# One level of Strassen's method in both feed-forward blocks of a two-layer encoder trunk

## The chip, the cores and the metric

The kernel runs on one core of one Trainium2 chip. The metric is the device time of one execution in microseconds (us); several executions are timed and their median is taken. Engines: PE (TensorE, matrix products; PEld is its weight load), DVE (VectorE), ACT (ScalarE), POOL (GpSimd) and SP (SyncE, which issues most transfers). Each engine takes its instructions in order, and waits for others by semaphores.

## The reference

`x` is 512 tokens of 1024 features, in float32. Two layers, each with two sub-layers, and each sub-layer does `x = x + RMSNorm_post(f(RMSNorm_pre(x)))`. The first sub-layer is a mixer (layer 0: forgetting attention and pooling; layer 1: a gated linear recurrence). The second one is the feed-forward block, and it is the one that changes:

```python
def swiglu(h, w_gate, w_up, w_down):
    return (jax.nn.silu(h @ w_gate) * (h @ w_up)) @ w_down
```

`w_gate` and `w_up` are 1024 x 2816, `w_down` is 2816 x 1024.

## The kernel before

One program, in the order mixer 0, feed-forward 0, mixer 1, feed-forward 1. Every float32 product a.b is carried as three products of a shorter type (float32r): ah.bh + ah.bl + al.bh, where ah holds the upper bits and al = a - ah the rest (`mm3`, L123 to L127). So each operand exists as a high and a low tile, and a third of a block product is one matrix instruction.

**Weights** stream from memory in units of [128, 1024] (512 KB), in the order of use. `unit()` (L153) hands out the next one and first has `prefetch` (L146) bring in two more. `split_weights` (L139) does it for one: SP issues the load into a `raw` buffer (three of them), ACT casts it into `whi`, DVE subtracts to get `wlo` (four pairs). These three are put ahead of other work in the scheduler (`tc.high_priority`). In the profile every DVE instruction stands under L89, the helper that records it.

**The activations** h lie transposed, as 8 tiles of features by 512 tokens, high (`hTh`) and low (`hTl`).

**Gate and up** (`ffn`, L689): 22 column tiles of 128 for each. The first four products run in halves of 256 tokens (`split_proj`, L674), since token blocks 2 and 3 come later from the mixer; the other 40 take 512 tokens, 8 k-steps of 3 instructions each. Per tile pair: Silu on ACT (L706), a product on DVE, a cast on ACT (L709) and a subtraction on POOL (L710) that makes the low part.

**Down**: 22 units; `TokenMajor` (L510) accumulates four token blocks by two halves of the features in the eight banks of PSUM. The last six units are held back and used token block by token block (`finish`), so that `Finish` (L556) can normalize one block while the next one is multiplied: `half` takes squares on ACT and scales on DVE, `block` takes the root on POOL (`pow`, L553), adds to x (`xres`), and does the next norm, which `second` and `transpose` queue behind a given amount of PE work (`later`, `tick`, L107 to L116). `need` forces them when their result is called for.

PE's order is the order of the program text, as those helpers leave it.

Of the kernel before, what the change touches and what calls it, by code (L numbers as in the profile page):

```python
# [7 lines left out]
F32 = mybir.dt.float32  # L8
# [13 lines left out]
FT = FF // P  # L22
EPS = 1e-6
# [3 lines left out]
# columns of the packed per-partition constants and parameters  # L27
# [23 lines left out]
# shape constants: identity | causal mask | zeros, upper triangle with the diagonal, ones  # L51
# [7 lines left out]
def tile_trunk(ctx: ExitStack, tc: tile.TileContext, cst_d, sh_d, xw_d, x_d, gains_d, pw_d, w_d, out_d):  # L59
    """Every float32 product a.b is carried as ah.bh + ah.bl + al.bh on float32r,  # L60
    where ah holds the top 12 bits of a and al = a - ah the rest, exactly."""
# [9 lines left out]
    def f32(ap):  # L71
        return ap.bitcast(F32)
# [6 lines left out]
    class Recorded:  # L79
        """an engine that remembers the last instruction given to it"""  # L80
# [21 lines left out]
    # work for the tensor engine that is queued behind `delay` us of other work of it,  # L102
    # while what it needs is being made
# [19 lines left out]
    def mm3(out, ah, al, bh, bl, start, stop, us=0.65):  # L123
        nc.tensor.matmul(out, lhsT=ah, rhs=bh, start=start, stop=False)  # L124
        nc.tensor.matmul(out, lhsT=ah, rhs=bl, start=False, stop=False)  # L125
        nc.tensor.matmul(out, lhsT=al, rhs=bh, start=False, stop=stop)  # L126
        tick(us)  # L127

# [4 lines left out]
    NU = w_d.shape[0]  # L133
# [5 lines left out]
    def split_weights(src, n, hi, lo):  # L139
        raw = pw.tile([P, D], F32, name="raw", tag="raw", bufs=3)  # L140
        with tc.high_priority():
            nc.sync.dma_start(out=raw[:, :n], in_=src)
            nc.scalar.copy(out=hi, in_=raw[:, :n])  # L143
            vec.tensor_sub(out=lo, in0=raw[:, :n], in1=f32(hi))

    def prefetch(n):  # L146
        while state["loaded"] < min(NU, state["used"] + n):
            hi, lo = place.get(state["loaded"], whl)()
            split_weights(w_d[state["loaded"]], D, hi, lo)
            ready.append((hi, lo))  # L150
            state["loaded"] += 1

# [27 lines left out]
    # the tensor engine's clock rises while the first loads are under way  # L180
# [9 lines left out]
    def log1p(out, e, u, d):  # L190
        """out = log(1 + e) for 0 <= e <= 1, with what the rounding of 1 + e takes off; u and d are scratch."""
# [7 lines left out]
    # ================= layer 0 mixer =================  # L199
# [4 lines left out]
    # values and forget gates, k outermost, on x*g; the row scale is applied on the way out.  # L204
    # columns: even heads, gates | odd heads
# [4 lines left out]
    for k in range(KT):  # L210
        xw = pw.tile([P, T + 520], F32, name="raw", tag="raw", bufs=3)
# [36 lines left out]
    # row scale of the first norm  # L248
# [41 lines left out]
    # -8 softplus(-lam)  # L290
# [4 lines left out]
    # c = cumsum(log f), as rows 32*b + 4*h + r for every b and r, by a product with the triangle  # L295
# [10 lines left out]
    def gates():  # L306
# [12 lines left out]
        # c[t] - c[s] as the product of rows c_hi[t], c_lo[t], 1, 1 and 1, 1, -c_hi[s], -c_lo[s]  # L319
# [40 lines left out]
    split_weights(pw_d, T, pwt[:, 0], pwt[:, 1])  # L360
# [106 lines left out]
    def transposes(pr):  # L467
        # s blocks 0 | 1 | zeros, 3, 2 of the transposed probabilities
# [19 lines left out]
    def values(h, parts):  # L488
# [8 lines left out]
        # the products of the values' low parts lie on the other half of the partitions  # L497
# [12 lines left out]
    class TokenMajor:  # L510
        """out[t, :] += a[k].T @ w[k] over the k of `srcs`; one bank per (token block, half of the features)."""
# [43 lines left out]

    class Finish:  # L556
        """Post-norm, residual, next pre-norm and its transpose, a token block at a time."""

        def __init__(self, n):
            self.gpost = gtile()  # L560
            nc.sync.dma_start(out=self.gpost, in_=gains_d[2 * n:2 * n + 1, :].broadcast_to([P, D]))
            self.gpre = None
            if n < 3:
# [4 lines left out]
        def half(self, i, hf, acc):  # L568
            if hf == 0:
                self.u[i] = (small(2), tmp())  # L570
            ss, u = self.u[i]
            cs = slice(hf * T, (hf + 1) * T)
            nc.scalar.activation(out=junk[:, cs], in_=acc, func=AF.Square, scale=1.0 / 32, accum_out=ss[:, hf:hf + 1])  # L573
            vec.tensor_mul(out=u[:, cs], in0=acc, in1=self.gpost[:, cs])

        def block(self, i):
# [27 lines left out]
            def transpose():  # L604
                h = box["h"]
# [292 lines left out]
```

## Time and profile before

| what | us |
|---|---|
| runs | 1100.03, 1100.60, 1099.24 |
| median | 1100.03 |
| span of the profiled execution, first to last instruction | 1097.0 |
| what lies around that span, by the median | 3.0 |
| PE busy | 1079.5 (98%) |
| PE weight loads, beside the products | 893.5 |
| DVE busy | 485.1 (44%) |
| ACT busy | 421.3 (38%) |
| POOL busy | 139.7 (13%) |

The share of busy time says which engine has no room left; the chain of waits says what the end hung on. A PE row in the timeline gives its start and its own duration; rows overlap in the pipeline, so the cost of one instruction is the distance between starts. The granted clock of PE is 0.997 of its upper level (2.4 GHz) over the span.

### The profile page before, as it was taken

The page shows a single profiled execution, that of the slowest core. Times are in us where ns is not written, and L with a number is a line of the kernel's source. Part 1 is how long each engine was busy: PE and PEld are TensorE (multiplying, and loading weights), DVE is VectorE, ACT ScalarE, POOL GpSimd, SP SyncE. Part 2 cuts the span into 40 slices and gives each one's busy share as a digit, 9 for nine tenths or more (in the row PEclk, how much of TensorE's full clock was granted, in tenths as well). Part 3 has the DMA queues.
Part 4 walks back from the last instruction along what each step waited for, and adds up shares of the span by engine and source line. Part 5 has one row for each costly group of instructions (what it writes and reads, how often), then busy time and mean ns, then how long its engine had stood idle before and what let it go on. Part 6 is the DMA issues. An engine that isn't in the chain of part 4 may idle for free.

```text
span 1097.0 us, 12987 instructions
## 1 busy us (share of the span) xinstructions
PE 1079.5 (98%) x5166; PEld 893.5 (81%) x5166; DVE 485.1 (44%) x665; ACT 421.3 (38%) x659; POOL 139.7 (13%) x140
## 2 busy tenths in 40 slices
PE   8999999999999999999999999999999999999997
PEld 7878787988888888888898887898888888888885
DVE  4899856522222222224348598543222222222323
ACT  6767634422222222114235984433222222221211
POOL 0020201111111111000003104101111111110000
PEclk9999999999999999999999999999999999999999
DMA  8644343322222222226113223313222222223401
GB/s 287 179 112 106 97 155 114 115 95 90 90 93 95 96 96 96 96 96 193 57 39 116 96 86 106 116 40 130 89 92 94 96 96 96 96 81 111 135 24 72
DMA packets 33292, 114.37 MB, mean 104 GB/s; under 512 B 4048, under 2 KB 4048, under 8 KB 33232
## 3 DMA queue, kind: packets, MB, share of 16 engines
q1 hardware_dynamic: 32656, 111.45, 31.1%
q10 hardware_dynamic: 576, 2.10, 0.5%
q8 instruction: 40, 0.66, 0.2%
q14 instruction: 20, 0.16, 0.0%
HBM read 107.24 MB, written 2.10 MB: 100 GB/s over the span
## 4 chain that ended last, share of the span: by engine, by line
PE 83%; DVE 8%; ACT 3%; issue 2%; DMA 2%; POOL 0%; SPq 0%; DVEq 0%; POOLq 0%; ACTq 0%
PE ps L125 27%; PE ps L124 27%; PE ps L126 27%; DVE wlo L89 2%; DVE tmp L89 2%; DVE cr L89 2%; DVE th L89 1%; ACT whi L143 1%; PE ps L610 1%; DMA tmp<-in_sh 1%; PE ps L475 1%; PE ps L495 1%; ACT th L774 1%; PE ps L447 0%; DMA raw<-in_xw 0%
## 5 line engine op out<-in xcount | busy, mean ns | idle before, releaser
L124 PE MATMUL ps<-hTh,whi 128*128 128x512 f32 (+1 forms) x1024 | 382.8, 375 | 0.2 <-DVE vs L89 0.2
L125 PE MATMUL ps<-hTl,whi 128*128 128x512 f32 (+1 forms) x1024 | 382.4, 374 | 0.0
L126 PE MATMUL ps<-hTh,wlo 128*128 128x512 f32 (+1 forms) x1024 | 382.4, 374 | 0.0
L143 ACT CAST whi<-raw 128x1024 fp32r<-128x1024 f32 x160 | 167.6, 1048 | 471.5 <-issue 176.2
L89 DVE TENSOR_TENSOR wlo<-raw,whi 128x1024 fp32r<-128x1024 f32 (+1 forms) x168 | 204.3, 1216 | 321.5 <-ACT whi L143 315.8
L126 PEld LDWEIGHTS ps<-hTh,wlo 128*128 128x128 f32 x1024 | 192.9, 188 | 36.6
L125 PEld LDWEIGHTS ps<-hTl,whi 128*128 128x128 f32 x1024 | 192.9, 188 | 36.3 <-issue 0.2
L124 PEld LDWEIGHTS ps<-hTh,whi 128*128 128x128 f32 x1024 | 192.5, 188 | 36.6 <-PE ps L126 0.4
L710 POOL TENSOR_TENSOR gT<-tmp,gT 128x512 fp32r<-128x512 f32 x44 | 78.4, 1781 | 407.1 <-ACT gT L709 407.1
L126 PE MATMUL ps<-whi,gT 128*128 128x512 f32 x256 | 99.6, 389 | 0.0
L124 PE MATMUL ps<-whi,gT 128*128 128x512 f32 x256 | 99.6, 389 | 0.0
L125 PE MATMUL ps<-wlo,gT 128*128 128x512 f32 x256 | 99.6, 389 | 0.0
L89 DVE TENSOR_TENSOR tmp<-tmp,ps 128x512 f32<-128x512 f32 x44 | 30.3, 688 | 144.0 <-PE ps L126 142.6
L553 POOL TENSOR_TENSOR small<-small,nhalf 128x1 f32<-128x1 f32 x28 | 15.4, 551 | 331.0 <-DVE small L89 328.4
L126 PEld LDWEIGHTS ps<-whi,gT 128*128 128x128 f32 x256 | 48.1, 188 | 10.1
L125 PEld LDWEIGHTS ps<-wlo,gT 128*128 128x128 f32 x256 | 48.1, 188 | 10.0
L124 PEld LDWEIGHTS ps<-whi,gT 128*128 128x128 f32 x256 | 48.1, 188 | 10.0
L89 DVE TENSOR_TENSOR tmp<-ps,gain 128x512 f32<-128x512 f32 x32 | 21.9, 690 | 55.5 <-ACT junk L573 55.4
L573 ACT ACTIVATE junk<-ps 128x512 bf16<-128x512 f32 x32 | 19.0, 596 | 62.0 <-PE ps L126 61.7
L124 PE MATMUL ps<-gT 128*128 128x512 f32 x96 | 37.5, 391 | 0.0
L126 PE MATMUL ps<-gT 128*128 128x512 f32 x96 | 37.4, 389 | 0.0
L125 PE MATMUL ps<-gT 128*128 128x512 f32 x96 | 37.4, 389 | 0.0
(179 smaller groups left out, 1108.3 us busy)
## 6 DMA issues: line engine op xcount, KB each, us to landing
raw<-in_w SPq DMA_DIRECT2D x180, 512.0 KB, 3.5
gain<-in_gains SPq DMA_DIRECT2D x7, 512.0 KB, 3.5
raw<-in_xw SPq DMA_DIRECT2D x6, 516.0 KB, 6.3
big<-in_x ACTq DMA_DIRECT2D x4, 512.0 KB, 6.9
big<-big SPq DMA_DIRECT2D x16, 128.0 KB, 2.6
xres<-in_x SPq DMA_DIRECT2D x4, 512.0 KB, 4.7
out_dram<-xres SPq DMA_DIRECT2D x3, 512.0 KB, 2.6
big<-tmp SPq DMA_DIRECT2D x8, 128.0 KB, 3.1
```

The lines of the kernel that those rows point to most:

```text
L89: self.last = fn(*a, **k)
L124: nc.tensor.matmul(out, lhsT=ah, rhs=bh, start=start, stop=False)
L125: nc.tensor.matmul(out, lhsT=ah, rhs=bl, start=False, stop=False)
L126: nc.tensor.matmul(out, lhsT=al, rhs=bh, start=False, stop=stop)
L143: nc.scalar.copy(out=hi, in_=raw[:, :n])
L475: nc.tensor.transpose(tp[:, b * P:(b + 1) * P], pr[i][:, j * P:(j + 1) * P], ident)
L495: nc.tensor.matmul(acc[:, dst], lhsT=v, rhs=parts[g][q][:, src], start=j == 0 and q == 0, stop=j == 3 and q == 1)
L553: nc.gpsimd.tensor_tensor(out=r, in0=ms, in1=nhalf[:, :1], op=ALU.pow)
L573: nc.scalar.activation(out=junk[:, cs], in_=acc, func=AF.Square, scale=1.0 / 32, accum_out=ss[:, hf:hf + 1])
L610: nc.tensor.transpose(tp[:, b * P:(b + 1) * P], h[:, k * P:(k + 1) * P], ident)
L710: nc.gpsimd.tensor_sub(out=v[:, 1], in0=g, in1=f32(v[:, 0]))
L774: tanhs.append(nc.scalar.activation(out=th[m], in_=ra[m], func=AF.Tanh, scale=coef[:, m:m + 1]))
```

## The change

Each of the four big products of a feed-forward block (gate and up together, and down) is cut into two by two blocks: tokens 0-255 and 256-511, features of the inner dimension in two halves, columns in two halves. The eight products of blocks are made by seven (Winograd's form), from sums of blocks of the activations (S1 to S4) and of the weights.

- **Weight sums.** `add_to` adds one raw weight block to another, in place, on GpSimd: four per column pair in gate and up (11 pairs), and three per down unit (six, the last of half the size). The sequence of a pair is W11, then q5 = W11 + W12', p6 = q5 + W22' and q4 = p6 + W21' in the one buffer `v`, and p7 = W12' + W22' in another (the signs are put into the weights by the host). Every sum is split into high and low after it is made, and before the next sum goes into the same buffer. For down, the sums p6 are stored to a scratch in memory and loaded again for q4, which is added on DVE. There are six `raw` buffers in place of three.
- **Gate and up.** Seven products of a column pair, each 24 instructions per half of 256 columns (gate, up): 168 instructions of 256 columns for a pair. Merges: five sums on DVE with PSUM, four Silu, four products on DVE. Three pairs (`LEAD`) start with the two products on tokens 0-255 alone, before the blocks S1 to S4 are there.
- **Activation sums.** `Blocks.put` makes them from the transposed tiles at the end of a mixer; with token blocks 2 and 3 it takes nine DVE instructions a block in place of two.
- **Down.** Three stages: A uses units p1, q5, p6; B W22 and W21; C p7 and q4. The gated activations and their sums are split into high and low by `form` (ACT, DVE) as the stages need them. The two last q4 units are used token block by token block.
- `in_dn` holds the down weights as blocks of 512 columns, so that a row of a load has 2 KB.

```diff
+NP = FT // 2
+DU = (NP + 1) // 2
+LEAD = 3
+RAW = 6
+    def add_to(acc, other, eng):
+        with tc.high_priority():
+            eng.tensor_add(out=acc, in0=acc, in1=other)
...
+        for j in range(LEAD):
+            recipes.append(lambda j=j: load(j, 0))
+            recipes.append(lambda j=j: load(j, 3))
...
+            def q5(j=j, st=st):
+                if j < LEAD:
+                    p1(j, st)
+                st["12"] = load(j, 1)
+                add_to(st["v"], st["12"], nc.gpsimd)
+                return st["v"]
...
+            def p7(j=j, st=st):
+                add_to(st["12"], st["22"], nc.gpsimd)
+                return st["12"]
...
+            recipes.extend([q5, p6, p7, lambda st=st: st["22"], q4] if j < LEAD
+                           else [p1, q5, p6, p2, p7, lambda st=st: st["22"], q4])
...
+        def q4(u):
+            v = rawtile(sums[u], sums[u].shape[-1])
+            add_to(v, load(3, u), vec)
+            return v
...
+    class Blocks:
...
+            nc.scalar.copy(out=x22, in_=tv[1])
+            vec.tensor_sub(out=s1, in0=tv[0], in1=x22)
+            split(S1, s1)
+            vec.tensor_sub(out=s2, in0=s1, in1=x11)
+            split(S2, s2)
+            vec.tensor_sub(out=s3, in0=x11, in1=tv[0])
+            split(S3, s3)
+            vec.tensor_add(out=s1, in0=s2, in1=x12)
+            split(S4, s1)
+            split(A22, x22)
...
+        need(0, 1)
+        for j in range(LEAD):
+            led.append(first(j))
+            second(j, led[j][0])
+        need(2, 3)
+        for j in range(NP):
+            b1, y = led[j] if j < LEAD else first(j)
+            z, c = hx[:, j % 2, :T], hx[:, j % 2, T:]
+            b3 = ps()
+            gate_product(b3, unit(), S1)
+            b2 = ps()
+            gate_product(b2, unit(), S2)
+            vec.tensor_add(out=y, in0=b2, in1=y)
+            vec.tensor_sub(out=z, in0=b3, in1=y)
+            if j >= LEAD:
+                second(j, b1)
+            b4 = ps()
+            gate_product(b4, unit(), S3)
+            vec.tensor_sub(out=c, in0=z, in1=b4)
+            gated(j, 3, c, c[:, :256])
...
+        for u in range(DU):
+            if u % 2 == 0:
...
+                vec.tensor_sub(out=t, in0=g21, in1=g22)
+                f5.append(form(t))
+                vec.tensor_sub(out=g21, in0=g11, in1=g21)
+                vec.tensor_sub(out=g11, in0=t, in1=g11)
+                f6.append(form(g11))
+            down_product(b1, unit(), u, f1)
+            down_product(b3, unit(), u, f5)
+            down_product(b2, unit(), u, f6)
...
+        for u in range(DU):
+            if u % 2 == 0:
+                g11, g21, g12, g22 = (gs[u // 2][:, f] for f in range(4))
+                at = 4 if u // 2 != 1 else 6
+                f7.append(form(g21, at))
+                f4.append(form(g22, at + 1))
+            down_product(b7, unit(), u, f7)
+            if u < DU - 2:
+                down_product(b4, unit(), u, f4)
...
-        pre = split_proj(4)
-        for m in range(FT):
...
-        tail = 6
...
-        tm.finish(range(NB), fin)
```

The rows that follow are the order of instructions on one engine; in them `g0` to `g2` are the gated activations, `hTl` and `up1` the low parts of the block operands, `raw` a weight buffer, `small` the column of a norm.

**At the start of feed-forward 0, on DVE.** Before, the end of mixer 0:

```order
L89 SCALAR_TENSOR_TENSOR xres<-tmp,small,xres 128x512 x2
L89 TENSOR_TENSOR hTl<-ps,hTh 128x512
L89 SCALAR_TENSOR_TENSOR small<-small 128x1
L89 SCALAR_TENSOR_TENSOR tmp<-xres,small,gain 128x512 x2
L89 TENSOR_TENSOR hTl<-ps,hTh 128x512 x3
L89 TENSOR_TENSOR wlo<-raw,whi 128x1024
```

Now, from the two splits ahead of the norm of token block 3 to the first low parts of S1 and S2, which belong to token block 2:

```order
L101 TENSOR_TENSOR wlo_2260<-raw_2261,whi_2259 128x1024
L101 TENSOR_TENSOR wlo_2321<-raw_2322,whi_2320 128x1024
L101 SCALAR_TENSOR_TENSOR small_2186<-small_2124 128x1
L101 SCALAR_TENSOR_TENSOR tmp_2190<-xres_1836,small_2188,gain_1828 128x512 x2
L101 TENSOR_TENSOR g0_2135<-tmp_2196,ps_2138 128x256
L101 TENSOR_TENSOR tmp_2219<-ps_2209,tmp_2219 128x512
L101 TENSOR_TENSOR tmp_2220<-hx_70,ps_2209 128x512
L101 TENSOR_TENSOR tmp_2220<-tmp_2219,hx_70 128x512
L101 TENSOR_TENSOR wlo_2356<-raw_2322,whi_2355 128x1024
L101 TENSOR_TENSOR hTl_69<-tmp_2219,hTh_68 128x4x128
```

Two weight splits now stand ahead of the norm's `small`, and the sums and splits of blocks follow it. On POOL, the root of that norm (`small_2188`) now stands behind a weight sum:

```order
L689 TENSOR_TENSOR small_2122<-small_2120,nhalf_72 128x1
L166 TENSOR_TENSOR raw_2322<-raw_2322,raw_2357 128x1024
L689 TENSOR_TENSOR small_2188<-small_2186,nhalf_72 128x1
L166 TENSOR_TENSOR raw_2488<-raw_2488,raw_2490 128x1024
L166 TENSOR_TENSOR raw_2322<-raw_2322,raw_2453 128x1024
```

**From gate and up to down, on DVE.** Before, there is nothing but the weights' low parts and one product per tile:

```order
L89 TENSOR_TENSOR tmp<-tmp,ps 128x512
L89 TENSOR_TENSOR wlo<-raw,whi 128x1024 x2
L89 TENSOR_TENSOR tmp<-tmp,ps 128x512
L89 TENSOR_TENSOR wlo<-raw,whi 128x1024 x12
L89 TENSOR_TENSOR gT<-raw,gT 128x1024
```

Now (`raw_4757` is the buffer of the down unit u = 1, of which p1, q5 and p6 are split in turn):

```order
L101 TENSOR_TENSOR wlo_4756<-raw_4757,whi_4755 128x1024
L101 TENSOR_TENSOR y_4522<-ps_4618,y_4522 128x512
L101 TENSOR_TENSOR g0_2135<-tmp_4727,g0_2135 128x1024
L101 TENSOR_TENSOR g2_2137<-y_4522 128x256
L101 TENSOR_TENSOR tmp_4851<-g1_2136 128x1024
L101 TENSOR_TENSOR wlo_4774<-raw_4757,whi_4773 128x1024
L101 TENSOR_TENSOR hTl_69<-g0_2135,hTh_68 128x1024
L101 TENSOR_TENSOR hTl_69<-tmp_4851,hTh_68 128x1024
L101 TENSOR_TENSOR wlo_4793<-raw_4757,whi_4792 128x1024
```

The low part of the operand of p6 of u = 0 (`hTl_69<-g0_2135`) stands behind the split of q5 of u = 1.

**At the start of stage C, on DVE.** Before, the place that does the same work:

```order
L89 TENSOR_TENSOR gT<-raw,gT 128x1024 x5
L89 TENSOR_TENSOR wlo<-raw,whi 128x1024 x4
L89 TENSOR_TENSOR tmp<-ps,gain 128x512 x2
L89 SCALAR_TENSOR_TENSOR small<-small 128x1
L89 SCALAR_TENSOR_TENSOR xres<-tmp,small,xres 128x1024
```

Now:

```order
L101 TENSOR_TENSOR up1_2134<-g0_2135,up0_2133 128x1024
L101 TENSOR_TENSOR wlo_5354<-raw_5355,whi_5353 128x1024
L101 TENSOR_TENSOR wlo_5375<-raw_5376,whi_5374 128x1024
L101 TENSOR_TENSOR tmp_5318<-ps_4719,gain_5313 128x512
L101 TENSOR_TENSOR raw_5432<-raw_5432,raw_5434 128x1024
L101 TENSOR_TENSOR tmp_5318<-tmp_5318,gain_5313 128x512
L101 SCALAR_TENSOR_TENSOR small_5324<-small_5317 128x1
L101 TENSOR_TENSOR tmp_5332<-ps_5087,hx_70 128x512
L101 SCALAR_TENSOR_TENSOR xres_1830<-tmp_5318,small_5326,xres_1830 128x1024
L101 TENSOR_TENSOR up1_2134<-g0_2135,up0_2133 128x1024
```

The first row is the operand of p7, the last one that of q4; between them stand splits, a sum of weights and the norm of token block 0.

## Rows read from the trace of the kernel before

**Rows 1.** The page: the span, PE's busy time, the chain that ended last.

```profile
span 1097.0 us, 12987 instructions
PE 1079.5 (98%) x5166; PEld 893.5 (81%) x5166; DVE 485.1 (44%) x665; ACT 421.3 (38%) x659; POOL 139.7 (13%) x140
PE 83%; DVE 8%; ACT 3%; issue 2%; DMA 2%; POOL 0%; SPq 0%; DVEq 0%; POOLq 0%; ACTq 0%
```

**Rows 2.** Stretches: length, busy us (instructions) of each engine, PE clock, DMA share, GB/s.

```profile
214.00:437.00 223.00, 223.00 (x962) 180.83 (x961) 62.78 (x60) 62.87 (x80) 35.63 (x20) 1.00 0.29 97
437.00:553.90 116.90, 116.90 (x522) 96.77 (x521) 40.98 (x44) 32.40 (x43) 4.52 (x6) 1.00 0.33 104
969.40:1089.30 119.90, 119.90 (x530) 99.01 (x528) 32.69 (x33) 25.09 (x34) 3.45 (x4) 1.00 0.25 84
```

**Rows 3.** PE timeline, feed-forward 0: start, duration, engine, line, operation, out<-in.

```profile
189.32 0.28 PE L124 MATMUL ps<-hTh,whi 128*128 128x256 f32 x1
...
195.60 0.28 PE L126 MATMUL ps<-hTh,wlo 128*128 128x256 f32 x1
...
201.75 0.36 PE L124 MATMUL ps<-hTh,whi 128*128 128x256 f32 x1
...
213.89 0.28 PE L126 MATMUL ps<-hTh,wlo 128*128 128x256 f32 x1
214.01 0.40 PE L124 MATMUL ps<-hTh,whi 128*128 128x512 f32 x1
...
437.10 0.40 PE L124 MATMUL ps<-whi,gT 128*128 128x512 f32 x1
...
523.97 0.39 PE L126 MATMUL ps<-whi,gT 128*128 128x512 f32 x1
```

**Rows 4.** Groups by line and shape: count, busy us, mean ns, idle time before.

```profile
L89 DVE TENSOR_TENSOR wlo<-raw,whi 128x1024 fp32r<-128x1024 f32 x160 | 198.7, 1242 | 321.0 <-ACT whi L143 315.8
L143 ACT CAST whi<-raw 128x1024 fp32r<-128x1024 f32 x160 | 167.6, 1048 | 471.5 <-issue 176.2 <-PE ps L125 171.0 <-PE ps L126 120.0
L89 DVE TENSOR_TENSOR tmp<-tmp,ps 128x512 f32<-128x512 f32 x44 | 30.3, 688 | 144.0 <-PE ps L126 142.6 <-ACT tmp L706 1.4
L553 POOL TENSOR_TENSOR small<-small,nhalf 128x1 f32<-128x1 f32 x28 | 15.4, 551 | 331.0 <-DVE small L89 328.4 <-PE ps L610 2.6
L89 DVE SCALAR_TENSOR_TENSOR xres<-tmp,small,xres 128x1024 f32<-128x1024 f32 x12 | 15.4, 1285 | 7.8 <-POOL small L553 7.8
L710 POOL TENSOR_TENSOR gT<-tmp,gT 128x512 fp32r<-128x512 f32 x44 | 78.4, 1781 | 407.1 <-ACT gT L709 407.1
L403 POOL TENSOR_TENSOR tmp<-tmp 128x510 f32<-128x510 f32 x2 | 2.1, 1036 | 5.3 <-issue 5.3
```

**Rows 5.** Timelines of POOL and DVE where an instruction of each overlaps.

```profile
126.12 1.41 POOL L403 TENSOR_TENSOR tmp<-tmp 128x511 f32<-128x511 f32 x1 [1.84 <-DVE tmp L89]
597.81 1.30 POOL L755 TENSOR_TENSOR hl<-cr,hl 128x512 fp32r<-128x512 f32 x1 [0.48 <-ACT hl L754]
...
125.96 0.68 DVE L89 TENSOR_TENSOR tmp<-tmp 128x510 f32<-128x510 f32 x1
126.55 2.06 DVE L89 TENSOR_TENSOR wlo<-raw,whi 128x1024 fp32r<-128x1024 f32 x1
598.72 1.47 DVE L89 TENSOR_TENSOR wlo<-raw,whi 128x1024 fp32r<-128x1024 f32 x1 [1.64 <-ACT whi L143]
```

**Rows 6.** Two stretches at the start where the DMA engines are full; columns as in rows 2.

```profile
5.00:6.00 1.00, 0.00 (x0) 0.00 (x0) 0.57 (x1) 0.58 (x1) 0.00 (x0) 1.00 1.04 321
14.00:16.00 2.00, 2.00 (x19) 2.00 (x18) 0.00 (x0) 0.08 (x1) 0.00 (x0) 1.00 1.02 408
```

**Rows 7.** DVE timeline before feed-forward 0: norm and transposed tiles of token block 3.

```profile
196.78 1.41 DVE L89 SCALAR_TENSOR_TENSOR xres<-tmp,small,xres 128x512 f32<-128x512 f32 x2 [0.73 <-POOL small L553]
199.87 1.41 DVE L89 SCALAR_TENSOR_TENSOR tmp<-xres,small,gain 128x512 f32<-128x512 f32 x2 [0.67 <-POOL small L553]
202.12 1.29 DVE L89 TENSOR_TENSOR hTl<-ps,hTh 128x512 fp32r<-128x512 f32 x2 [0.24 <-ACT hTh L613]
```

**Rows 8.** Stretches of 1 us after PE's last product; columns as in rows 2.

```profile
1092.00:1093.00 1.00, 0.00 (x0) 0.00 (x0) 1.00 (x2) 0.00 (x0) 0.00 (x0) 1.00 0.00 0
1093.00:1094.00 1.00, 0.00 (x0) 0.00 (x0) 0.12 (x1) 0.00 (x0) 0.00 (x0) 0.80 0.67 260
1094.00:1095.00 1.00, 0.00 (x0) 0.00 (x0) 0.00 (x0) 0.00 (x0) 0.00 (x0) 0.50 0.69 264
```

More of the change, by code (lines that the diff above doesn't have):

```diff
@@ L712, in ffn @@
[L712 to L721 removed]
+        upper[:] = [pf.tile([P, KT // 2 * D], F32R, name=f"up{n}") for n in range(2)]
@@ new lines, in ffn, with form, down_product @@
+        turn = [7, A11, S1, S2, A12, S3, S4, A22]
+        turns = [0]
+        def form(src, at=None):
+            if at is None:
+                at = turn[turns[0] % 8]
+                turns[0] += 1
+            n = src.shape[-1]
+            hi, lo = (a[:, :n] for a in slot(at))
+            nc.scalar.copy(out=hi, in_=src)
+            vec.tensor_sub(out=lo, in0=src, in1=f32(hi))
+            return hi, lo
+        def down_product(banks, w, u, fs, blocks=(0, 1), more=False):
+            wh, wl = w
+            for a in blocks:
+                for kk in range(2 if u < DU - 1 else 1):
+                    k = 2 * u + kk
+                    fh, fl = fs[k // 4]
+                    ts = slice(k % 4 * 256 + a * P, k % 4 * 256 + a * P + P)
+                    cs = slice(kk * T, kk * T + T)
+                    mm3(banks[a], fh[:, ts], fl[:, ts], wh[:, cs], wl[:, cs], not more and k == 0, k == NP - 1, 0.70, more)
@@ new lines, in ffn @@
+        y = [ytile(), ytile()]
+        z = [hx[:, 0, :T], hx[:, 0, T:]]
+        for a in range(2):
+            nc.scalar.copy(out=y[a], in_=b1[a])
+            vec.tensor_add(out=y[a], in0=b2[a], in1=y[a])
+            vec.tensor_sub(out=z[a], in0=b3[a], in1=y[a])
+        b5 = pair()
+        f2, f3 = [], []
+        for u in range(DU):
+            if u % 2 == 0:
+                g11, g21, g12, g22 = (gs[u // 2][:, f] for f in range(4))
+                f2.append(form(g12))
+                vec.tensor_add(out=g12, in0=g11, in1=g12)
+                f3.append(form(g12))
+            down_product(b5, unit(), u, f3)
+            down_product(b1, unit(), u, f2, more=True)
@@ new lines, in ffn @@
+        fin = Finish(1 if layer == 0 else 3, Plain())
+        for a in range(2):
+            fin.half(a, 0, b1[a])
+            fin.half(a, 1, None, lambda out, a=a: vec.tensor_add(out=out, in0=b5[a], in1=z[a]))
+            fin.block(a)
+        b7, b4 = pair(), pair()
+        f7, f4 = [], []
+        last = []
+        for u in range(DU):
+            if u % 2 == 0:
+                g11, g21, g12, g22 = (gs[u // 2][:, f] for f in range(4))
+                at = 4 if u // 2 != 1 else 6
[4 more added lines that the diff above has]
+                down_product(b4, unit(), u, f4)
@@ L722, in ffn @@
+        for a in range(2):
+            fin.half(2 + a, 1, None, lambda out, a=a: vec.tensor_sub(out=out, in0=z[a], in1=b7[a]))
+            vec.tensor_add(out=y[a], in0=b7[a], in1=y[a])
+        ws = [unit(), unit()]
+        for a in range(2):
+            for n, u in enumerate((DU - 2, DU - 1)):
+                down_product(b4, ws[n], u, f4, blocks=(a,))
+            fin.half(2 + a, 0, None, lambda out, a=a: vec.tensor_add(out=out, in0=b4[a], in1=y[a]))
+            fin.block(2 + a)
         st.close()
```

240 lines of the change are left out of this document (186 added, 54 removed).

## The prediction

> **What bounds the kernel now.** I read the page first. PE is busy for 1079.5 of 1097.0 us, and the chain that ended last lies on PE for 83% [rows 1]: whatever shortens PE's work shortens the kernel, as long as nothing new makes PE wait. Then the stretches: in gate and up (214 to 437 us) and in down, PE has no gap at all, while DVE works for 62.78 of 223 us, ACT for 62.87, POOL for 35.63, and DMA for a third [rows 2]. So there is room on the other engines as a mean; what has to be asked is whether each sum comes in time. The span is 3.0 us under the median of the runs; the sum is made against the span, and the same 3.0 added at the end.
>
> **What PE saves.** From starts of rows [rows 3]: gate and up in 512 columns took 437.10 - 214.01 = 223.09 us for 960 instructions, 0.2324 each. In 256 columns, 54 instructions from 189.32 to 195.60 took 0.1185 each, and 102 from 201.75 to 213.89 0.1202. Down took 0.2268 each (384 from 437.10 to 523.97).
> - Gate and up before: 960 x 0.2324 + 192 x 0.120 = 246.1. After: 11 pairs x 168 = 1848 instructions of 256 columns, by 0.1195 (between the two rows): 220.8. That is -25.3 a block, between -23.9 (0.1202) and -27.1 (0.1185).
> - Down: 528 instructions become 462 of the same size: 66 x 0.2268 = -15.0.
> - Both blocks: 2 x 40.3 = **-80.6**. Were PE never to wait, the median would be 1019.
>
> **The price of what is added.** A weight sum reads two float32 operands of 1024 and writes one. No row has it. The nearest is the POOL sum of 510 columns of the same types, 1.036 [rows 4]: twice that is 2.07, and I take 2.0. Dearer is the POOL subtraction of 512 columns into the shorter type, 1.30 beside little else [rows 5]: 2.6. The mean of those in the feed-forward block, 1.781 [rows 4], holds waits for DVE; twice that, 3.56, is the far end.
>
> POOL and DVE also exclude each other. The split at 598.72 took 1.47, against 1.242 as a mean [rows 4], and ended at 600.19, 1.08 after the POOL subtraction had ended (597.81 + 1.30); the split at 126.55 took 2.06 and ended 1.08 after POOL's sum (126.12 + 1.41) [rows 5]. So a DVE instruction with both operands in SBUF waits for the whole POOL one, and then takes 1.08. The other way round, that POOL sum ended 0.90 after the DVE instruction ahead of it (125.96 + 0.68): after a wait, twice 0.90 gives 1.8 for a sum. DVE instructions on PSUM I take as free of this.
>
> The Trainium skill (GPSIMD Engine Reference, 3.1 and 4.1) speaks against the change: it gives 4497 ns to a float32 add of 2048 on GpSimd, 1.96 times VectorE's, and puts elementwise adds on VectorE. By it a sum of 1024 would take 2.25 (an estimate); at 0.25 more for each of two sums in five units of stage A, and of two blocks, the forecast would be 5 us higher.
>
> **Gate and up, in their middle: nothing.** PE needs 168 x 0.1195 = 20.1 us for a pair. DVE has 7 splits x 1.242, 5 merges x 0.688 [rows 4] and 4 products of half that size, about 0.41: 13.8. POOL's four sums take 7.2 to 8. Wholly one after the other they would need 21 to 22, but merges can run beside sums, and splits after a wait are shorter: 7 x 1.08 + 3 x 0.3 + 4 x 1.8 = 15.7 for what excludes each other. Weights are split three products (8.6 us) ahead of use. I count 0, with up to 0.9 a pair, 10 a block, as the dear end.
>
> **Start of gate and up: +11 and +5.5.** Token block 3's norm was ready in 199.87 + 1.41, and its transposed tiles by 203.4, hidden behind products of blocks 0 and 1 [rows 7]. Now its root stands behind a sum in POOL's queue (2.0), and two splits stand ahead of it on DVE (2 x 1.24), each with casts or loads to wait for: 4 to 6 us later, and PE's queue reaches the transposes in order. Behind them come some 15 DVE instructions of 0.69 each until S1 is whole, 10 to 11, with 2 to 3 for sums that exclude them. Against it stand the remaining lead products, 2.25 x 24 x 0.1195 = 6.4. So 5 + 10.5 + 2 - 6.4 = 11; 9 to 16. In feed-forward 1 fewer splits stand ahead (2 to 3 us late) and three products (8.6) cover: 2.5 + 10.5 + 2 - 8.6 = 6, taken as 5.5; 4 to 10.
>
> **Stage A of down: +15.5 each.** p1, q5 and p6 of a unit share one buffer, so their work is a chain: split 1.23; twice sum 1.8, cast 1.05, split 1.23 [rows 4]. That is 9.4, and the next unit's first split stands behind it in DVE's order. `form` instructions (1.2 each, some eighteen over six units) stand between, and take the port before a sum: 10 to 12, taken as 11. PE needs 36 x 0.2268 = 8.16. Five units x 2.8 = 14, and 1.5 at the start, where the low part of p6's operand stands behind the split of the second unit's q5, and comes about 11 us after gate and up have ended, with 8.4 of products ahead. If POOL always went first: 9.4 - 8.16 = 1.2 by five, and 1, so 7. High end 20.
>
> **Stage B: 0.** Loads and splits alone, as before.
>
> **Stage C: +9 each.** The first operand of p7 goes into a place that the last product of B reads: cast 1.05 and subtraction 1.2 lie bare, 2.3. The operand of q4 stands behind `xres` of block 0, which waits for a root that stands behind a sum in POOL's queue (2.0 + 0.55), and behind a sum on DVE: 1.2 + 1.285 + 0.69, less 0.4 of cover, +5.3 [rows 4]. Then loads: four of 512 KB in each 24 x 0.2268 = 5.44 us are 385 GB/s. Full DMA engines moved 408 in one stretch and 321 in another [rows 6]: by the first nothing, by the second 1.1 a unit, 6 in all; with what six buffers hold ahead I take 1.4. From 6 to 14.
>
> **Ends: +3 and +1.** Token blocks 2 and 3 now finish together, with splits ahead of their merges: 3 before mixer 1, 1 before the last store.
>
> **Sum.** Waits: 11 + 15.5 + 9 + 3 = 38.5, and 5.5 + 15.5 + 9 + 1 = 31: 69.5. -80.6 + 69.5 = -11.1: span 1085.9, median **1089**. I add nothing for PE's clock: it read 1.00 up to 1093 us and 0.50 from 1094, PE having done nothing since its last product at 1089 [rows 8]. The longest single waits could meet the lower level; 0 to 8 us, kept for the range.
>
> **Rivals.**
> 1. *POOL gets its turn first, and PE's queue finds other products.* Stage A costs 7 to 8 and stage C 6, the starts 8 and 4, the ends 2: 2 x 7.5 + 2 x 6 + 12 + 2 = 41; 1097 - 80.6 + 41 + 3 = **1060**. For it: POOL idles for 87% [rows 1], and a queue that is always ready takes the port as soon as a split ends. Against it: DVE in stage A has next to no gap. Chance 0.18.
> 2. *The sum costs 2.6* (the row at 597.81). Then a pair needs 15.7 + 4 x 0.8 = 18.9 for what excludes each other, and with the merges that sit at the head of DVE's queue 0.7 more than PE: 0.7 x 16 pairs behind the lead = 11; stage A 2 x 0.65 x 5 x 2 = 13; the starts 4; stage C 2. Together +30: **1119**, slower than before. It decides from about 2.3, where the 11 us are eaten (4 x 0.4 leaves a pair just covered, and the other places cost 0.6 of their 19). For it: the fp32 sum was seen alone but twice. Against: it has the very types of the 1.036 row. With 3.56 POOL itself is nearly enough to fill a pair (14.2 of 20.1, and DVE's 9.9 beside it), and the time passes 1190. Chance 0.22.
> 3. *No wait at all*: 1019 to 1035. Against it are the chains above, whose lengths come from rows. Chance 0.03.
>
> **How the numbers follow.** My forecast has 0.57, from 1070 to 1105 by its own bounds (stage A 7 to 20, C 6 to 14, starts 13 to 26). Range **1048 to 1122**: it takes in most of rivals 1 and 2, and leaves out the cases without waits and with a sum over 2.7. A measurement can tell 0.2%, 2.2 us, from no change. Slower by more: rival 2 above its deciding point and the top of my own range, 0.23. Same: 0.05. Faster: 0.72.
>
> **What would show it.** PE's instructions of 256 columns at 0.1185 to 0.1202 over 11 pairs, and 20 to 20.3 us a pair; PE's busy time falling by about 80; waits in three places of each block (start, stage A, start of C), of 5 to 16 us each, released by DVE's low parts, and none in stage B. A sum on POOL of 1.8 to 2.1. I am wrong if a sum is above 2.4, if pairs in the middle take over 20.6, or if stage A's waits are under 7 or over 20 a block.

## The result, and the profile after

The change is slower: a median of 1173.5 us (1171.5 to 1174.3, 4 runs) against 1099.7; the ratio is 1.067, interval 1.065 to 1.068. The forecast was 1089, range 1048 to 1122. The side was wrong: the second rival had it (a GpSimd sum dearer than 2.3 us), at 1119, still 54 us too low.

The page of the change: the span, busy times, the chain that ended last, and the groups of the weights' work (count, busy us, mean ns, idle time before).

```profile
span 1172.5 us, 16474 instructions
PE 1058.0 (90%) x6426; PEld 929.6 (79%) x6426; DVE 896.4 (76%) x1055; ACT 562.9 (48%) x857; POOL 386.6 (33%) x220
...
issue 12%; POOL 10%; PE 8%; DVE 5%; DMA 1%; ACT 1%; POOLq 0%; DVEq 0%; ACTq 0%
...
L101 DVE TENSOR_TENSOR wlo<-raw,whi 128x1024 fp32r<-128x1024 f32 (+2 forms) x286 | 403.7, 1426 | 148.2 <-ACT whi L161 147.2
L166 POOL TENSOR_TENSOR raw<-raw 128x1024 f32<-128x1024 f32 (+1 forms) x124 | 320.5, 2586 | 426.9 <-DVE wlo L101 316.8
L161 ACT CAST whi<-raw 128x1024 fp32r<-128x1024 f32 (+1 forms) x278 | 281.3, 1023 | 366.4 <-POOL raw L166 239.9
```

PE is no longer full (98% in [rows 1], 90% here), and of the chain that could be followed back the largest share of an engine is POOL's. A sum takes 2.586 us as a mean, where the forecast put 2.0, and a split 1.426 in place of 1.242 [rows 4]. The casts (`L161`) waited 240 us for sums. PE's mean clock is 0.956.

Stretches of the change, in the columns of [rows 2]: some five and a half of the eight pairs of gate and up behind the lead, stage A, the first three quarters of stage B's products, the rest of B with stage C, all of feed-forward 0.

```profile
325.10:441.80 116.70, 114.44 (x938) 112.04 (x937) 86.46 (x91) 50.68 (x69) 54.39 (x22) 1.00 0.30 94
451.60:519.80 68.20, 54.60 (x200) 40.67 (x199) 60.55 (x45) 27.48 (x32) 31.22 (x11) 0.90 0.47 153
519.80:542.30 22.50, 22.50 (x98) 17.97 (x97) 18.07 (x18) 12.22 (x15) 3.20 (x1) 1.00 0.70 234
542.30:602.60 60.30, 45.81 (x186) 36.31 (x185) 41.67 (x49) 25.75 (x38) 15.30 (x9) 0.89 0.66 224
```

DVE is busy for 60.6 of the 68.2 us of stage A, and part of that is waiting: DVE counts as busy while POOL holds it off. The timelines of POOL and of DVE in a pair of gate and up show it.

```profile
351.93 2.52 POOL L166 TENSOR_TENSOR raw<-raw 128x1024 f32<-128x1024 f32 x1 [2.42 <-DVE wlo L101]
...
352.10 0.68 DVE L101 TENSOR_TENSOR y<-ps,y 128x512 f32<-128x512 f32 x1
352.70 2.83 DVE L101 TENSOR_TENSOR wlo<-raw,whi 128x1024 fp32r<-128x1024 f32 x1
```

The sum ends at 354.45, the split at 355.53: 1.08 later, as in [rows 5]. The merge from PSUM in between took its ordinary 0.68 under the sum. The Trainium skill (SBUF — State Buffer, section "SBUF: two separate sides") has it that a GpSimd operation and a VectorE one with two SBUF inputs lock each other out for a whole instruction; these rows agree. The Trainium skill's GPSIMD Engine Reference (3.1) led to an estimate of 2.25 for a sum; the quarter of the sums that met the least delay took up to 2.41. That estimate was nearer than the row that I chose.

In stage A a sum also stands back for VectorE:

```profile
479.13 1.21 DVE L101 TENSOR_TENSOR up<-g,up 128x1024 fp32r<-128x1024 f32 x1
...
479.28 3.31 POOL L166 TENSOR_TENSOR raw<-raw 128x1024 f32<-128x1024 f32 x1 [2.90 <-DVE wlo L101]
```

The subtraction is one of `form`; the sum ended 2.25 us after it. Of the 18 whole sums of the two stages A, 14 took 3.0 to 3.3 us.

Where the 75.5 us of the span went. "Bare" is the number of instructions times the spacing of [rows 3]; B is here 132 instructions of down after A, C the last 132. "No sums" is e2_no_sums below.

| stretch, us | bare | change, block 0 / 1 | no sums, block 0 / 1 |
|---|---|---|---|
| mixer 0 | 189.3 (before) | 201.1 | 194.5 |
| gate and up | 220.8 | 250.4 / 245.6 | 229.8 / 228.6 |
| stage A | 44.9 | 68.5 / 68.5 | 45.7 / 45.7 |
| stage B | 29.9 | 37.6 / 37.0 | 34.5 / 34.3 |
| stage C | 29.9 | 45.2 / 38.6 | 38.9 / 34.5 |

PE's saving was there: the bare span is 1097.0 - 80.6 = 1016.4. Waits of 156 us took its place, where I had 69.5: 54 in gate and up (forecast 16.5), 47 in stage A (31), 15 in B (0), 24 in C (18), 12 in mixer 0 (0), and 4 in mixer 1 and at the end (4).

### The profile page after: what moved, and what is told of

It reads as the page before. It is cut to its first block, busy times and chain, and to the rows that moved or that the text cites. A ratio compares the mean times of both kernels' runs of the same rounds, so it can differ in the third digit from the quotient of the medians.

```text
span 1172.5 us, 16474 instructions
## 1 busy us (share of the span) xinstructions
PE 1058.0 (90%) x6426; PEld 929.6 (79%) x6426; DVE 896.4 (76%) x1055; ACT 562.9 (48%) x857; POOL 386.6 (33%) x220
## 5 line engine op out<-in xcount | busy, mean ns | idle before, releaser
L101 DVE TENSOR_TENSOR wlo<-raw,whi 128x1024 fp32r<-128x1024 f32 (+2 forms) x286 | 403.7, 1426 | 148.2 <-ACT whi L161 147.2
L166 POOL TENSOR_TENSOR raw<-raw 128x1024 f32<-128x1024 f32 (+1 forms) x124 | 320.5, 2586 | 426.9 <-DVE wlo L101 316.8
L161 ACT CAST whi<-raw 128x1024 fp32r<-128x1024 f32 (+1 forms) x278 | 281.3, 1023 | 366.4 <-POOL raw L166 239.9
L137 PE MATMUL ps<-hTh,whi 128*128 128x256 f32 (+1 forms) x960 | 298.8, 312 | 14.2 <-ACT y L917 11.0
L139 PE MATMUL ps<-hTh,wlo 128*128 128x256 f32 (+1 forms) x960 | 298.1, 311 | 9.0 <-DVE wlo L101 9.0
L138 PE MATMUL ps<-hTl,whi 128*128 128x256 f32 (+1 forms) x960 | 294.1, 307 | 5.0 <-DVE hTl L101 5.0
L137 PE MATMUL ps<-up,whi 128*128 128x256 f32 x528 | 149.7, 284 | 1.9 <-DVE hx L101 1.8
L138 PE MATMUL ps<-up,whi 128*128 128x256 f32 x528 | 149.4, 283 | 0.0
L139 PE MATMUL ps<-up,wlo 128*128 128x256 f32 x528 | 149.3, 283 | 0.0
L137 PEld LDWEIGHTS ps<-up,whi 128*128 128x128 f32 x528 | 101.1, 192 | 2.7 <-issue 2.7
L138 PEld LDWEIGHTS ps<-up,whi 128*128 128x128 f32 x528 | 101.2, 192 | 0.0
L137 PE MATMUL ps<-whi,up 128*128 128x512 f32 x180 | 79.4, 441 | 22.0 <-ACT up L963 13.1
L139 PE MATMUL ps<-whi,up 128*128 128x512 f32 x180 | 77.6, 433 | 6.9 <-DVE up L101 6.9
```

The lines of the kernel that those rows point to most:

```text
L101: self.last = fn(*a, **k)
L161: nc.scalar.copy(out=hi, in_=raw)
L166: eng.tensor_add(out=acc, in0=acc, in1=other)
```

## The experiments

Theory: the time of a GpSimd sum and its exclusion of VectorE set the waits. Rivals: VectorE's own queue, the loads, PE's clock. Each time is that of one execution, beside the kernel before at 1097 to 1101 us, unless more are named.

**e1_sums_dve: the sums on VectorE.** In all seven places where GpSimd was named:

```diff
-                add_to(st["v"], st["12"], nc.gpsimd)
+                add_to(st["v"], st["12"], vec)
```

> The change with every weight sum on VectorE instead of GpSimd. Theory (the time of a GpSimd sum, 2.43 us in the trace of the change against the 2.0 of the forecast, and its exclusion of VectorE set the waits): a sum on VectorE takes about 1.25 us, VectorE then has 13.8 + 4 x 1.25 = 18.8 us of work for a column pair of 20.1, nothing excludes it, so pairs of gate and up run at 20.1 to 20.3 us in place of 20.9 and stage A of down shortens by 8 to 15 us each: 1125 to 1145 us. Rival (VectorE's own in-order queue sets the waits, and more work in it makes them worse): pairs over 21 us, stage A at 70 us or more, 1180 to 1210 us.

Measured 1114.45: 59 us less, further than the theory had it (stage A is 12.8 us shorter, as it had it), and the rival falls. The groups of the weights' work on its page:

```profile
L101 DVE TENSOR_TENSOR wlo<-raw,whi 128x1024 fp32r<-128x1024 f32 (+2 forms) x286 | 336.2, 1187 | 77.8 <-ACT whi L161 76.7 <-ACT whi L357 0.5
L101 DVE TENSOR_TENSOR raw<-raw 128x1024 f32<-128x1024 f32 (+1 forms) x136 | 161.2, 1187 | 15.1 <-DMA raw<-in_dn 12.9 <-DMA raw<-in_w 1.0 <-DVE wlo L101 0.8
```

The sum takes half as long, and the split is back at 1.187: 286 x (1.426 - 1.187) = 68 us of VectorE's time had been waiting, by these means. The busy time of DVE rose only from 896 to 915. A pair of gate and up starts at 330.75 and the next at 350.69, so 19.9 us; in the change 346.03 and 366.92, so 20.9. Stretches of this run, pairs and stage A:

```profile
322.10:422.00 99.90, 99.90 (x844) 99.90 (x843) 86.57 (x101) 45.74 (x62) 0.00 (x0) 1.00 0.33 106
430.40:486.10 55.70, 49.26 (x201) 36.15 (x200) 53.38 (x54) 27.88 (x32) 0.00 (x0) 1.00 0.59 181
```

In these pairs PE has no gap. In stage A DVE works 53.4 of 55.7 us: it is the bound there, 10.9 us over the bare 44.9.

**e2_no_sums: no GpSimd sums.**

```diff
-            eng.tensor_add(out=acc, in0=acc, in1=other)
+            if eng is vec:
+                eng.tensor_add(out=acc, in0=acc, in1=other)
```

> The change without its GpSimd weight sums: the loads stay, each product takes the unsummed block, so the result lacks these sums. Theory (sums and exclusion set the waits): pairs at 20.1 to 20.2 us, stage A of down near 48 us in place of 68.2, time 1085 to 1115. Rival (VectorE's queue and the order of the forms set them): stage A stays above 60 us, time over 1140. Rival (the loads set them): no change in stage A and C, time over 1155.

Measured 1070.21, below the theory's range. So GpSimd's sums cost the change 103 us, of which by the table 38 are in gate and up, 46 in stage A, 16 in B and C, 7 in mixer 0, less 2 in mixer 1. The loads were the same, so they are not what makes these 103 us. The other 52 us over the bare span have nothing to do with GpSimd's sums; the longest waits among them are at the start of stage C (PE timeline of this run):

```profile
504.48 0.80 PE L137 MATMUL ps<-whi,up 128*128 128x512 f32 x1 [3.79 <-ACT up L964]
...
513.22 0.50 PE L139 MATMUL ps<-whi,up 128*128 128x512 f32 x1 [3.10 <-DVE up L101]
```

**e5_sum768: sums at the forecast's price.** The sum over `acc[:, :768]`.

> The change with every GpSimd sum over three quarters of its columns (768 of 1024; the last quarter of the sum is left out). A sum then takes about 1.8 to 1.9 us, the price that the forecast gave to a whole one; all other instructions are as in the change. Theory A (the forecast failed by the price of the sum alone): its own time, 1089, at any rate 1070 to 1105. Theory B (other terms were short too: PE's clock after waits, the second products of the lead that wait for a copy, the end of mixer 0): 1105 to 1125, pairs of gate and up at 20.0 us, stage A at 50 to 57. Theory C (time follows the price in a line from 1070 without sums to 1172): 1145 to 1152.

Measured 1120.66, in the range of theory B, though stage A, at 59, is longer than it had it. Half of these sums took up to 1.96 us, the mean was 2.03:

```profile
L167 POOL TENSOR_TENSOR raw<-raw 128x768 f32<-128x768 f32 (+1 forms) x124 | 251.9, 2033 | 437.9 <-DVE wlo L101 332.2 <-DMA raw<-in_dn 70.0 <-DMA raw<-in_w 17.9
```

So the price of a sum was the larger part of my error (1173 to 1121). At that price the terms that hang on it came out near the forecast: every pair behind the lead took 19.95 us, and stage A was 14.1 and 14.4 us over its bare time (forecast 15.5). The 32 us from 1089 to 1121 lie elsewhere: the starts took 12 more than forecast, stages B and C together 14, mixer 0 11, while the pairs and stage A took some 4 less.

**e10_offchain, with its control e11_nosums_raw5: is it the chain or the exclusion?** The sums go to a tile that nobody reads:

```diff
-RAW = 6
+RAW = 5
...
-            eng.tensor_add(out=acc, in0=acc, in1=other)
+            eng.tensor_add(out=acc if eng is vec else scr[:, :acc.shape[-1]], in0=acc, in1=other)
```

> The change with its GpSimd sums written to a tile that nobody reads (five raw buffers for its room), so the splits take unsummed blocks and wait for no sum, while GpSimd does as many sums of the same size and holds VectorE off. Theory 1 (the exclusion is most of the price): 1125 to 1160, splits at a mean of 1.4 us as in the change. Theory 2 (the length of the chain is): 1070 to 1090, near e2_no_sums (1070.21). In between: both, in that proportion.

> e2_no_sums (1070.21) with five raw buffers in place of six: the control of e10_offchain. If the exclusion is what e10_offchain measures: 1066 to 1080. If the missing buffer makes its time: over 1110.

Measured 1146.25, and 1075.51 for the control. Sums for which no split waits cost 71 us over that control. The change is 98 over it, with six buffers in place of five, which here made the runs without sums differ by 5 us. On the page of e10_offchain the two groups hold each other off even more:

```profile
L101 DVE TENSOR_TENSOR wlo<-raw,whi 128x1024 fp32r<-128x1024 f32 (+2 forms) x286 | 449.3, 1577 | 51.8 <-ACT whi L161 51.5 <-PE ps L138 0.2
L166 POOL TENSOR_TENSOR scr<-raw 128x1024 f32<-128x1024 f32 (+1 forms) x124 | 353.7, 2853 | 377.9 <-DMA raw<-in_dn 177.2 <-DMA raw<-in_w 160.1 <-issue 36.3
```

Some of the 71 can be buffers that a late sum holds, and roots that stand behind sums in POOL's queue, which this run does not separate from the exclusion. But the length of the chain alone is not the cause. Against the control, 38 of the 71 us are in gate and up (18 of them in the pairs behind the lead, most of that in the last pair of each block, unlike the change) and 24 in stage A, where the change lost 46: there the chain still has a part of its own.

**e3_yorder: the lead reordered.** `first(j + 1)` is issued ahead of `second(j)`.

> The change with the lead of gate and up reordered: the first product of pair j + 1 is issued ahead of the second product of pair j. In the trace of the change PE is idle for 11.0 us over both blocks before second products, released by the copy of the first product's bank (y). Theory (that copy is a wait of its own on PE, which the forecast did not have): these 11 us go, and two or three falls of PE's clock with them: 1156 to 1166 us. Rival (the time until S1 is whole is set by VectorE, and PE only waits elsewhere for it): the waits move to the products on S1, 1170 to 1176 us.

Measured 1171.55, 2 us less and within the change's own four executions: the rival. Gate and up took 252.2 and 245.1 us, against 250.4 and 245.6. In feed-forward 0 the two waits for the copy (2.9 and 2.2 us) went, but S1 was not ready any earlier, and PE waited 7.7 us for that. In feed-forward 1 the edit did not take the wait away (5.9 us before, 6.9 now), so what it costs there is not shown.

**e4_warm: products on zeros in PE's waits.** PE's clock in stretches of 2 us of the change, at a wait in stage A:

```profile
460.00:462.00 2.00, 0.00 (x0) 0.00 (x0) 2.00 (x1) 0.76 (x1) 1.20 (x1) 1.00 0.54 210
462.00:464.00 2.00, 0.58 (x1) 0.50 (x2) 2.00 (x4) 1.54 (x3) 0.00 (x0) 0.52 0.77 210
464.00:466.00 2.00, 2.00 (x6) 1.60 (x5) 2.00 (x3) 0.84 (x1) 1.03 (x1) 0.50 0.14 52
466.00:468.00 2.00, 2.00 (x6) 1.52 (x6) 2.00 (x2) 0.00 (x0) 2.00 (x1) 0.50 0.00 0
...
470.00:472.00 2.00, 2.00 (x10) 1.64 (x9) 1.98 (x3) 1.05 (x1) 0.00 (x0) 1.00 0.99 303
```

PE stood still, its clock went from 1.00 (2.4 GHz) to 0.50 (1.2 GHz), and 6 instructions ran in 2 us in place of 10.

> The change with products on zeros (bf16, 512 columns, about 0.22 us each) put on PE in the places where it waits longest: at the starts of gate and up, in stage A, at the start of stage C, before the transposes of token block 3. The clock of PE read 0.50 in about a dozen and a half stretches of the change of some 3.4 us each, and by the rows some 41 us of PE's time went with them. Theory (the fall of the clock after a wait costs time of its own): the mean clock rises from 0.956 to over 0.98 and the time falls by 15 to 35 us, to 1140 to 1158. Rival (what the waits wait for is set by the other engines, so a faster PE only waits longer): the clock rises, the time stays within 6 us of the change or grows by the added products, 1168 to 1185.

Measured 1193.10, longer than either had it, with a clock of 0.968 where the theory wanted over 0.98. In the change PE's clock read 0.50 in nineteen stretches, the last one behind its last product, and was busy in them for 82 us; here in eleven, for 49 us. In each stage A three such stretches became one, and the stage took 71.9 us in place of 68.5. So a higher clock did not shorten it; but the added products, 77.5 us in all, are in the time as well, and what the clock costs by itself stays open.

**m0_raw6: the kernel before with six raw buffers.**

> The kernel before, with six raw buffers in place of three and the change's smaller scratch for dynamic transfers, nothing else. Mixer 0 ended at 189.3 us before, at 201 in the change and at 194.5 without its sums. Theory (weights that run six buffers ahead share the DMA engines with the first loads of mixer 0, so its first products wait): feed-forward 0 starts 3 to 6 us later than 189.3, and the time is 1100 to 1105. Rival (the block sums at the mixer's end cost it): feed-forward 0 starts within 1 us of 189.3, time 1097 to 1100.

Measured 1105.93 against 1097.40, 1 us above the theory's range. The edit has two parts, six buffers and the smaller scratch, which this run does not separate. Its page shows the first loads later (8.5 us, before 6.3), and PE's timeline a wait in the first products:

```profile
raw<-in_xw SPq DMA_DIRECT2D x6, 516.0 KB, 8.5
...
26.94 0.39 PE L125 MATMUL ps<-wlo,hTh 128*128 128x264 f32 x1 [2.97 <-DVE wlo L89]
```

Feed-forward 0 starts at 192.8, 3.5 late, and another 3.5 us go in mixer 1, where some 48 products of the recurrence's gates take 17.5 us in place of 14.1. Whether the buffers cost the change as much is not shown: its first loads take 8.6 us too, and without sums (e2_no_sums) feed-forward 0 begins 5.2 us late, but of the two mixers e9_dve_tags below, which leaves them three, shortened only the second.

**Towards a better version.** All with sums on VectorE, unless GpSimd is named. One kernel, c4_lead4, gave 1089.03 to 1096.23 in seven executions (six of them as c4_again), so a difference of a few us between single executions is not clear of noise.

e6_dve_formhi puts `form` under `tc.high_priority()`; e8_dve_swap takes other slots in stage C:

```diff
-                at = 4 if u // 2 != 1 else 6
+                at = 6 if u // 2 != 1 else 4
```

> Sums on VectorE as in e1_sums_dve (1114.45), and the operands that form makes at the same priority as weight splits. Theory (in stage A and at the start of C these operands stand behind splits that are not yet due): stage A 55.8 to about 50, the waits of 5.0 and 4.9 us at the start of stage C shorter: 1095 to 1108. Rival (in stage A VectorE is full, and the order changes nothing): 1112 to 1118.

> Sums on VectorE as in e1_sums_dve (1114.45), and the first operands of stage C in slots 6 and 7, which nothing reads in stage B, in place of 4 and 5, which its last product reads. Theory (the two waits at the start of stage C, 4.96 and 4.88 us, come from the slot and from what stands behind it in VectorE's queue): both go but for 1 to 3 us, with the clock's fall behind them, so 8 to 11 us a block, 1092 to 1100. Rival (the waits come from VectorE's queue, whatever the slot): 1108 to 1116.

Measured 1109.10 and 1111.48. In the first, the down products took 123 and 122 us in place of 133 and 131, but stage A took 57.3 (55.8 before the edit), and mixer 1 grew from 172.7 to 181.8, since the norms came later; the time lies between its theory and its rival. In the second, B fell from 35.7 and 34.3 to 30.6 (bare 29.9), and C rose from 41.5 and 40.4 to 44.9 and 42.4; the time is the rival's. In both the waits mostly moved on.

e9_dve_tags gives the feed-forward blocks three of the six raw buffers for themselves, and leaves the mixers three.

> Sums on VectorE (e1_sums_dve: 1114.45, feed-forward 0 from 194.6 us), and of the six raw buffers three belong to the feed-forward blocks alone, so the mixers have three as before the change. With six buffers in the kernel before, feed-forward 0 began 3.5 us late and the time was 8.5 us longer. Theory (in the mixers the early loads put weight splits ahead of the mixers' own work): feed-forward 0 starts at 190 to 191.5 us, mixer 1 is 2 to 4 us shorter, time 1106 to 1110. Rival (the end of the mixer, with its block sums, takes these microseconds): start at 193.5 or later, time 1112 to 1116.

Measured 1106.67, in the range, but not by the stated way: feed-forward 0 began at 196.2. Of its first loads the two of 260 KB took 5.6 us in place of 4.2, for a reason that I don't know, and the six of 516 KB 6.5 in place of 8.6. Feed-forward 0 was 3 us shorter, mixer 1 2.2, and the last block from gate and up to its end 4 us.

c2_combo is e9 with the slots, the lead's order and the priority for stage A's operands; c3_q5pool puts one sum of stage A back on GpSimd; c4_lead4 has `LEAD = 4`.

> Sums on VectorE, three of the raw buffers for the feed-forward blocks alone, the operands of stage A at the splits' priority, the first operands of stage C in slots 6 and 7, the lead's products reordered. If the parts add up: from 1114 some 6 for the buffers, 6 for stage A, 8 for stage C and the tail, 4 for the lead, so 1088 to 1094, faster than the kernel before. If the waits move on to the next thing that is late, as in e8_dve_swap, where stage B lost 4 to 5 us a block and stage C took most of them back: 1100 to 1108.

> c2_combo, with one of the two sums of a unit in stage A (q5) on GpSimd again. Theory (stage A on VectorE is bound by its amount of work, 9.9 us a unit against 8.3 of PE, and GpSimd's exclusion costs more than the 1.2 us it takes off): stage A is longer than in c2_combo by 2 to 6 us a block. Rival (VectorE's amount of work alone counts): stage A shorter by 3 to 6 us a block.

> c2_combo with a lead of four pairs in place of three: 5.7 us more of products that need no block of tokens 256 to 511 stand ahead of S1, and one more weight unit pair is loaded and split twice. Theory (the start of gate and up waits for the chain of token block 3 on VectorE): gate and up shorter by 3 to 6 us a block, time 6 to 12 us under c2_combo. Rival (the further splits on VectorE and the copies delay that chain by as much): within 3 us of c2_combo.

Measured 1102.15, 1120.36 and 1096.23: c2 in the range where the waits move on, c3 by more than its theory, c4 at the edge of its own (5.9 us under c2). In c3 stage A went from 56.2 to 63.8 us in both blocks: with 1.2 us of a unit's work off VectorE, it lost 7.6, the exclusion once more. Six of its ten whole sums took 5.0 to 5.3 us. The one at 453.81 overlapped three VectorE instructions that followed each other without a gap, and ended 2.26 us after the last of them:

```profile
453.81 5.32 POOL L173 TENSOR_TENSOR rawf<-rawf,raw 128x1024 f32<-128x1024 f32 x1 [9.23 <-DVE wlo L101]
...
453.65 1.22 DVE L101 TENSOR_TENSOR g<-g 128x1024 f32<-128x1024 f32 x1
454.78 0.95 DVE L101 TENSOR_TENSOR tmp<-g 128x768 f32<-128x768 f32 x1
455.65 1.22 DVE L101 TENSOR_TENSOR g<-tmp,g 128x1024 f32<-128x1024 f32 x1
```

In c4 gate and up fell from 238.5 and 233.7 to 236.1 and 229.8.

c4_again is c4 in six executions; c5_lead5 has a lead of five (and five raw buffers), in four executions; c6_pool is c4's layout with the sums on GpSimd; e12_dve_raw5 is e1 with five buffers.

> The kernel of c4_lead4 again, timed in five rounds beside the kernel before. One look gave 1096.23 against 1099.13, a ratio of 0.9974. If that was no chance: ratio 0.996 to 0.9985, its interval under 1. Otherwise the interval holds 1.

> c4_lead4 with a lead of five pairs, five y tiles, and five raw buffers in the feed-forward blocks (for room). A lead of four took 2.4 and 3.9 us off gate and up against three. If the start still waits for token block 3 (6.4 us of idle time before the first product on S1 in feed-forward 0), another 2 to 5 us a block: 1088 to 1093. If VectorE's splits of the further units delay that chain as much, or five buffers are too few: 1095 to 1102.

> The layout of c4_lead4 (three raw buffers of their own for the feed-forward blocks, reordered lead of four pairs, slots 6 and 7 first in stage C, operands of stage A at the splits' priority), with the sums on GpSimd as in the change. If the engine of the sums decides (59 us between the change and e1_sums_dve): 1145 to 1160. If the layout decides: under 1125.

> e1_sums_dve (1114.45) with five raw buffers in place of six. If c5_lead5 was slow for its missing buffer (loads that wait for a buffer to come free): 1135 to 1160. If it was slow for its lead: 1108 to 1122.

c4_again: 1091.95 (1089.03 to 1095.95) against 1098.8, ratio 0.994, interval 0.992 to 0.996: faster than the kernel before, by 0.6%. c6_pool: 1167.76; the layout is worth 6 us with sums on GpSimd, the engine 76 us. c5_lead5: 1130.19, ratio 1.027 (1.025 to 1.030), above both of its ranges. e12_dve_raw5: 1110.43, so five buffers in one pool do not explain that. Whether it is the lead of five, or the split of the buffers into three and two, stays open. The page of c4_again:

```profile
span 1087.2 us, 16435 instructions
PE 1025.8 (94%) x6426; PEld 908.6 (84%) x6426; DVE 912.6 (84%) x1179; ACT 567.0 (52%) x857; POOL 65.0 (6%) x96
```

PE has work for 54 us less than in [rows 1], and still 61 us of gaps: some 24 in stages A and C, 12 in gate and up, 17 in the mixers, 9 after its last product.

## Why the prediction was wrong, step by step

- **What PE saves: right.** Without waits a pair took 19.9 us (forecast 20.1), stage A of e2_no_sums 45.7 (44.9).
- **The price of a sum: the step that failed.** I doubled the row of 1.036 for 510 columns and took 2.0, since its types were the same, and gave 1.8 to a sum after a wait. It was 2.4 with little in its way and 2.59 as a mean. The other row, 1.30 for 512 columns [rows 5], doubled to 2.6, was the right one. I had it as rival 2 with a chance of 0.22, on the ground of its types; e5_sum768 prices that choice at 53 us. The ground was wrong too: a sum of 512 columns of the very types, with nothing of VectorE beside it, took 1.30 (c3_q5pool, 493.07).
- **"Gate and up, in their middle: nothing": wrong by the price.** I counted POOL's and VectorE's work as if each fitted into the other's gaps (15.7 of 20.1 us). With 2.03 a sum it did (e5_sum768: 19.95 us a pair). With 2.4 to 2.6 a sum it was 0.9 us a pair too much, the size that rival 2 gave (0.7). Of the 38 us that go with the sums in the two blocks' gate and up, 22 are in the pairs behind the lead, and 16 at the starts.
- **Stage A: mechanism right, size short.** Forecast 15.5, high end 20; measured 23.6 each. e2_no_sums has it at 0.8, so nearly all of it is the sums; e1_sums_dve at 10.9, there by VectorE's amount of work. For a sum after a wait I put 1.8; most in stage A took 3.0 to 3.3. That e5_sum768 came out near 15.5 is in part luck, since its sums in stage A took about 2.5.
- **Rival 2's own price was short.** It gave 2 x 6.5 us to stage A and 4 to the starts for a sum dearer by 0.65. It moved the sum and left the splits alone; but every sum also held off the split behind it (1.187 to 1.426), on the engine that had the least room.
- **Stages B and C.** B was put at 0, and is 7.4 longer than bare, 4.5 of it without GpSimd's sums. But in the table B runs to the start of C's first product, and nearly all of this is the wait for that product's operand (6.8 and 6.3 us in the change), which the forecast counted in C, at 2.3. The two stages together: forecast 18, measured 39, of which 23 without GpSimd's sums. The slot and VectorE's queue were named; in e8_dve_swap, with another slot, the wait before C went, and C itself grew.
- **Starts: too small.** 11 and 5.5 were forecast for the waits, sums included. Up to the first pair behind the lead, the change is 20 and 15 us over bare, e5_sum768 17 and 12, and e2_no_sums, without GpSimd's sums, still 10 and 9. I had not seen that PE's second products wait for a copy: 11 us of PE's idle time in the change. Taking 5 of them away won nothing clear of noise (e3_yorder).
- **Left out: mixer 0, and the raw buffers.** I put nothing to mixer 0, and feed-forward 0 began 11.8 us late, 6.6 of it with GpSimd's sums and 5.2 without. I costed six buffers in place of three at nothing; in the kernel before, with the smaller scratch, they cost 8.5 us, in both mixers.
- **PE's clock: 0 to 8.** PE was busy for 82 us at 1.2 GHz; at 2.4 GHz half of that would do, so the price is at most about 41 us (an estimate). How much of it lengthened the kernel stays open: filling some of the waits did not shorten it (e4_warm).

## What to carry to other kernels

Before work is moved to an idle engine, price it by the dearest row of its kind, and price what it does to the engine beside it as well: here GpSimd was idle for 87% of the time, and its sums made VectorE, the next bound, lose 68 us. An engine with room as a mean may have none where another engine holds it off; VectorE did the same sums in half the time and the kernel ran 59 us faster. A method that saves 7% of the bound engine's work is worth it only if operands come early: the version that beat the kernel before kept 7 of the 80 us.

## What the runs showed of the hardware

- A float32 sum on GpSimd: 2.4 us for 1024 columns and 1.85 for 768 where little delayed it, against about 1.2 for 1024 on VectorE (e1_sums_dve). A sum of 512 took 1.30 (c3_q5pool), which lies on that line; two rows of 1.036 for 510 columns in the kernel before do not, and I don't know why.
- A GpSimd sum that meets VectorE instructions without a gap between them can wait for several: 5.32 us behind three (c3_q5pool, 453.81).
- A merge on VectorE with one input in PSUM ran beside a GpSimd sum at its ordinary 0.68 us (352.10).
- PE's clock went to 1.2 GHz in a wait of 4.1 us, and read 2.4 GHz again from 470 us on, PE having been busy since 463.4 (the change).
- More buffers for loads can slow a kernel: six in place of three, with a smaller scratch for dynamic transfers, took the first loads from 6.3 to 8.5 us and the kernel from 1097 to 1106 (m0_raw6).
